# A hybrid encoder step in one core: transfers moved to GpSimd's queue, a third raw weight slot, and an input norm without GpSimd

## The chip, the cores and the metric

The kernel runs on one core of one Trainium2 chip. The core has a matrix engine (TensorE, "PE" in the profile, "PEld" its weight loads), VectorE (DVE), ScalarE (ACT), GpSimd (POOL) and SyncE (SP). Each of them takes its own instructions in order. Transfers between device memory and the core's on-chip memory are issued here from SP's and from POOL's instruction queues and run on 16 DMA engines. The metric is the device time of one execution in microseconds (us), as the median of several runs; lower is better.

## The reference

One layer of a streaming encoder, with the same weights for a prompt of 1024 frames and a sample of 32 frames. D is 1024, the MLP's hidden width 4096, the memory 256 tokens. Everything is float32.

```python
def trunk_layer(x, attn_core, conv_left, mem_k, mem_v, ...):
    h = rms_norm(x, g_mix)
    z = h @ w_in
    q, k, v, ch, cb, cc, ga, gb = jnp.split(z, SPLITS, axis=-1)
    a = attn_core(q, k, v) @ w_attn_out          # sliding window, sinks
    u = cc * ch
    ...                                          # conv: 3 taps over u
    bo = (cb * conv) @ w_conv_out
    x = x + (jax.nn.sigmoid(ga) * a + jax.nn.sigmoid(gb) * bo) @ w_mix_out
    hc = rms_norm(x, g_cross)
    cq = (hc @ w_cq).reshape(B, n, MEM_HEADS, MEM_HEAD_DIM)
    s = jnp.einsum('bqhd,bmhd->bhqm', cq, mem_k) * MEM_SCALE
    p = jax.nn.softmax(s, axis=-1)
    co = jnp.einsum('bhqm,bmhd->bqhd', p, mem_v).reshape(B, n, MEM_DIM)
    x = x + co @ w_co
    hm = rms_norm(x, g_mlp)
    x = x + jnp.square(jax.nn.relu(hm @ w_up)) @ w_down
    return x, k, v, up[:, -(CONV_WIDTH - 1):]
```

## The kernel before

The 1056 frames lie along the free axis in three chunks of 384, 384 and 288 (CH), the features along the partitions in eight tiles f of 128. Every float32 product is made of three matmuls: a weight is split into a high part `wh` (ACT, L119) and a low part `wl` (DVE, L120), activations into two such parts, and `gemm` (L175 to L177) sums high times high, high times low and low times high.

**Weights.** `fetch_w` (L135) loads the next weight in the program's list into one of two raw slots `wr` (SP, L137); `issue_w` (L141) splits it. For the weights in `kept`, the low part is also stored (`wl_d`, SP, L154) and loaded back (L148) for the next chunk.

**The start** is `norm_x`: x of the three chunks is loaded; `parts` makes X, the split of x times the norm's gain (`scaled_split`, ACT L255, DVE L256); `squares` sums the squares of the eight tiles in two halves, one on DVE (L313), one on POOL (L309 the squares of chunk 0, L313 the adds), and `column` merges them (L296). From the sums `chunk_col` makes the norm's factor per frame (L208 to L214), and `chunk_row` spreads it along the free axis (L222, L223, L225). K and V of a chunk are multiplied from X without the factor, then scaled (`v_scale`, L443, L412, L413). Then come Q of chunk 0 and the rest of attention. In the same time POOL starts the sums of w_down pieces (L739 load, L744 adds, L745 store), one after the other, up to 727 us.

**The trunk** (some 750 to 1080 us) goes chunk by chunk: `do_conv_out(c, f)` multiplies w_conv_out, loads the attention's part `m1` (SP) and adds it (L791); `do_mix(c, f)` loads x (L801, SP, into `ct`, a tag of six temporaries that many helpers share), multiplies w_mix and adds x (DVE, L805), makes the split of the sum (L255, L256) and its square (POOL L248, L252). The steps of cross-attention of the chunk before (scores, `turn`, `values` L916 to L931, `do_co` L943 to L947) and `normed_split` (L972, store L973) stand between the products of the next chunk.

**The MLP's up phase** (some 1080 to 1480 us). `up_part` multiplies one tile of w_up for one chunk, takes the positive part (DVE, L1000) and squares it (POOL, L1004). From 1220 us on `up_pair` makes a pair of tiles of chunks 0 and 1 by a Strassen-like scheme of fewer products: the sums of weights `s31` and `s24` are made on POOL (`pair_issue`, L1052 to L1055) and split (L119, L120); values are combined on POOL and DVE (L1111, L1136, L1145, L1154, L1162). Every value is put into the list `later`, and `flush` (L986) issues the stores on SP with the next product. In the down phase `pump` (L1206) and `refold` (L1217, L1221) load them again.

The order on each engine is made by a scheduler, which plays a timeline of the program and moves instructions within an engine; `pin` keeps some in the program's order, and within a `manual_schedule` block the order on the named engines is that of the code.

## Time and profile before

| | |
|---|---|
| runs | 1820.57, 1821.26, 1822.29 us (median 1821.26) |
| profiled execution | 1822.32 us |
| its span | 1820.5 us |
| TensorE busy | 1769.7 us (97%) |
| VectorE, ScalarE, GpSimd busy | 1110.2, 757.0, 531.4 us |
| mean granted TensorE clock | 0.99 |

The profile is of one execution; the span is from its first to its last recorded instruction. A row of a timeline has the start and the duration in us, the engine, the line, the operation and its tiles (out<-in), and in brackets the idle time before it with what ended it. A row of a group has the busy time and the mean in ns, then the idle time before the group. A row of waits has the total, the number and the longest, in us.

### The profile page before, as it was taken

How to read it: one execution, taken by the hardware profiler on the slowest of the kernel's cores; microseconds unless marked ns; L12 is line 12 of the kernel's file. 1: busy time of each engine (PE TensorE's matmuls, PEld its weight loads, DVE VectorE, ACT ScalarE, POOL GpSimd, SP SyncE). 2: the span in 40 equal slices, each digit the busy share in tenths (PEclk: the TensorE clock that was granted, in tenths of full speed). 3: DMA queues.
4: the chain of work that ended last, by engine and by line, in shares of the span. 5: the costliest groups of instructions: out<-in, count | busy, mean ns of one | idle time of the engine just before them, and what ended most of it. 6: DMA issues, size and time to landing. Idle time of an engine off the chain costs nothing. (4 is left out here: it accounts for less than half of the span.)

```text
span 1820.5 us, 29893 instructions
## 1 busy us (share of the span) xinstructions
PE 1769.7 (97%) x11172; PEld 1750.3 (96%) x11172; DVE 1110.2 (61%) x2083; ACT 757.0 (42%) x1486; POOL 531.4 (29%) x597
## 2 busy tenths in 40 slices
PE   7899999999999999999999989999999999999997
PEld 7899999999999999999999979999999999999997
DVE  7886766757665222425666768667566676436663
ACT  7553544535335210423465755632222343324453
POOL 4554310110113333002515142376544300100111
PEclk9999999999999999999999999999999999999999
DMA  6454411211126455516756657654334597446573
GB/s 224 161 175 150 149 56 53 80 56 63 61 93 199 148 174 183 163 55 210 242 197 214 225 191 251 241 189 140 133 125 138 160 295 223 156 128 205 193 241 105
DMA packets 166305, 293.35 MB, mean 161 GB/s; under 512 B 16624, under 2 KB 128016, under 8 KB 166032
## 3 DMA queue, kind: packets, MB, share of 16 engines
q1 hardware_dynamic: 156944, 257.88, 42.9%
q0 software_dynamic: 9216, 33.56, 5.2%
q8 instruction: 88, 1.44, 0.4%
q14 instruction: 57, 0.47, 0.1%
HBM read 217.89 MB, written 73.48 MB: 160 GB/s over the span
## 5 line engine op out<-in xcount | busy, mean ns | idle before, releaser
L175 PE MATMUL acc<-X,wh 128*128 128x384 f32 (+1 forms) x1200 | 392.1, 327 | 11.3 <-ACT wh L119 8.3
L176 PE MATMUL acc<-X,wh 128*128 128x384 f32 (+1 forms) x1200 | 389.0, 324 | 3.9 <-DVE X L256 3.9
L177 PE MATMUL acc<-X,wl 128*128 128x384 f32 (+1 forms) x1200 | 388.1, 323 | 0.4 <-DVE wl L120 0.4
L119 ACT CAST wh<-wr 128x1024 fp32r<-128x1024 f32 x208 | 218.2, 1049 | 361.1 <-PE acc L176 177.0
L120 DVE TENSOR_TENSOR wl<-wr,wh 128x1024 fp32r<-128x1024 f32 x208 | 274.3, 1319 | 99.8 <-ACT wh L119 98.7
L175 PEld LDWEIGHTS acc<-X,wh 128*128 128x128 f32 x1200 | 227.4, 189 | 12.0 <-ACT wh L119 8.3
L176 PEld LDWEIGHTS acc<-X,wh 128*128 128x128 f32 x1200 | 227.5, 190 | 4.9 <-DVE X L256 4.2
L177 PEld LDWEIGHTS acc<-X,wl 128*128 128x128 f32 x1200 | 227.2, 189 | 1.0 <-DVE wl L120 0.9
L175 PE MATMUL acc<-Y,wh 128*128 128x384 f32 (+1 forms) x624 | 202.4, 325 | 0.7 <-DVE ct L1000 0.4
L177 PE MATMUL acc<-Y,wl 128*128 128x384 f32 (+1 forms) x624 | 201.9, 324 | 0.0
L176 PE MATMUL acc<-Y,wh 128*128 128x384 f32 (+1 forms) x624 | 201.7, 323 | 0.0
L252 POOL TENSOR_TENSOR xacc<-xacc,ct 128x384 f32<-128x384 f32 (+1 forms) x62 | 76.5, 1237 | 319.3 <-ACT ct L250 314.2
L175 PEld LDWEIGHTS acc<-Y,wh 128*128 128x128 f32 x624 | 117.0, 188 | 1.4 <-DVE ct L1000 0.6
L176 PEld LDWEIGHTS acc<-Y,wh 128*128 128x128 f32 x624 | 117.1, 188 | 0.0
L177 PEld LDWEIGHTS acc<-Y,wl 128*128 128x128 f32 x624 | 117.1, 188 | 0.0
L1363 PE MATMUL acc<-Y,wh 128*128 128x384 f32 (+1 forms) x352 | 113.2, 322 | 1.3 <-DVE lt L1145 0.7
L1364 PE MATMUL acc<-Y,wh 128*128 128x384 f32 (+1 forms) x352 | 113.3, 322 | 0.6 <-DVE Y L120 0.6
L1365 PE MATMUL acc<-Y,wl 128*128 128x384 f32 (+1 forms) x352 | 113.0, 321 | 0.0
L119 ACT CAST PTh<-pt 128x512 fp32r<-128x512 f32 (+3 forms) x94 | 46.2, 516 | 124.5 <-PE pt L550 117.1
L120 DVE TENSOR_TENSOR Y<-ct,Y 128x384 fp32r<-128x384 f32 (+1 forms) x128 | 66.2, 549 | 42.3 <-ACT Y L119 42.1
L119 ACT CAST Y<-ct 128x384 fp32r<-128x384 f32 (+1 forms) x128 | 58.8, 486 | 59.0 <-DMA ct<-b_d 14.9
L1004 POOL TENSOR_TENSOR ct<-ct 128x288 f32<-128x288 f32 (+1 forms) x48 | 44.8, 934 | 120.3 <-DVE ct L1000 49.8
(309 smaller groups left out, 4192.5 us busy)
## 6 DMA issues: line engine op xcount, KB each, us to landing
wr<-in_w_in SPq DMA_DIRECT2D x50, 512.0 KB, 3.4
wr<-in_w_up SPq DMA_DIRECT2D x48, 512.0 KB, 3.9
wr<-in_w_down SPq DMA_DIRECT2D x32, 512.0 KB, 3.7
wr<-wsum_d SPq DMA_DIRECT2D x32, 512.0 KB, 3.5
wl<-wl_d SPq DMA_DIRECT2D x28, 512.0 KB, 4.8
wr<-in_w_conv_out SPq DMA_DIRECT2D x24, 512.0 KB, 4.2
wr<-in_w_mix SPq DMA_DIRECT2D x24, 512.0 KB, 4.2
ct<-b_d SPq DMA_DIRECT2D x48, 192.0 KB, 4.4
```

What stands on the lines that cost most here:

```text
L119: act.copy(hi, src)
L120: dve.tensor_sub(lo, src, hi.bitcast(F32))
L175: pe.matmul(out, wh[:, a], hi, start=(k == 0), stop=False)
L176: pe.matmul(out, wh[:, a], lo, start=False, stop=False)
L177: pe.matmul(out, wl[:, a], hi, start=False, stop=(k == len(acts) - 1))
L252: pool_e.tensor_tensor(acc, acc, sq, op=ALU.add)
L1004: pool_e.tensor_tensor(h, t, t, op=ALU.mult)
L1363: pe.matmul(a, wh[:, s], hi, start=(start and k == 0), stop=False, skip_group_check=True)
L1364: pe.matmul(a, wh[:, s], lo, start=False, stop=False, skip_group_check=True)
L1365: pe.matmul(a, wl[:, s], hi, start=False, stop=(stop and k == len(acts) - 1), skip_group_check=True)
```

## The change

Five things are changed. (a) Stores of the kept low parts go to POOL's queue. (b) The loads of m1 and x in the trunk go to POOL's queue, into four slots of their own (`ld`), and are asked for two products ahead (`add_next`). (c) Every third trunk weight goes into a third raw slot `wr3`. (d) At the start, all squares are on ACT (tag `sq`) and all adds on DVE (L307); ACT's and DVE's order for chunk 0 is written out, with the squares after the weights; splits of the later chunks are pinned; the scaling of a chunk's K and V comes after the next chunk's first V block, and that of the last chunk (`end`) after Q's first chunk. (e) Stores of `normed_split` and of `flush` go to POOL's queue. The numbers of lines in the changed kernel are up to 20 higher.

```diff
--- before.py
+++ after.py
@@ -129,10 +129,15 @@
             src = src[j]
         return src
 
-    fetched = []
+    fetched, trunk_raw, X = [], [0], {}
 
     def fetch_w():
-        raw = wp.tile([P, 1024], F32, tag="wr", bufs=2, name=nm("wr"))
+        name = worder[wpos[0] + len(fetched)][0]
+        trunk_raw[0] = trunk_raw[0] + 1 if name in ("w_conv_out", "w_mix", "w_cq", "w_co") else 0
+        if trunk_raw[0] % 3 == 1 and name in ("w_conv_out", "w_mix") and X:
+            raw = X["cr"].tile([P, 1024], F32, tag="wr3", name=nm("wr"))
+        else:
+            raw = wp.tile([P, 1024], F32, tag="wr", bufs=2, name=nm("wr"))
         src = weight(worder[wpos[0] + len(fetched)])
         sp.dma_start(raw.rearrange("p (i c) -> p i c", i=4) if len(src.shape) == 3 else raw, src)
         fetched.append(raw)
@@ -151,7 +156,7 @@
             split(hi, lo, raw)
             if key in kept:
                 kept[key] = dram.tile([P, 1024], F32, name=nm("wl_d"))
-                sp.dma_start(kept[key], lo.bitcast(F32))
+                pool_e.dma_start(kept[key], lo.bitcast(F32))
         ready.append((worder[wpos[0]], (hi, lo)))
         wpos[0] += 1
 
@@ -251,9 +256,9 @@
         if f:
             pool_e.tensor_tensor(acc, acc, sq, op=ALU.add)
 
-    def scaled_split(hi, lo, x, g):
-        act.mul(hi, x, col(g))
-        dve.scalar_tensor_tensor(lo, x, col(g), hi.bitcast(F32), op0=ALU.mult, op1=ALU.subtract)
+    def scaled_split(hi, lo, x, g, pinned=lambda x: x):
+        pinned(act.mul(hi, x, col(g)))
+        pinned(dve.scalar_tensor_tensor(lo, x, col(g), hi.bitcast(F32), op0=ALU.mult, op1=ALU.subtract))
 
 
     x_cm, xpool = opened("xpool", bufs=16)
@@ -264,6 +269,7 @@
         return st.tile([P, NF * 384], dt, tag="raw", bufs=3, name=nm("raw"))
 
     xg = [[None] * NF for _ in CH]
+    start_end = []
 
     def norm_x():
         pool_e.memset(ones, 1.0)
@@ -286,69 +292,72 @@
                     fetch_w()
                 raws.append(raw)
 
-        def parts(c, fs):
+        def parts(c, fs, pinned=lambda x: x):
             for f in fs:
                 xg[c][f] = (slot(xpool, f"X{c}", CH[c][1]), slot(xpool, f"X{c}", CH[c][1]))
-                scaled_split(*xg[c][f], raws[c][:, f], G_MIX + f)
-
-        def column(c):
-            a, b = accs[c]
-            dve.tensor_add(a, a, b)
-            accs[c] = [a]
-            chunk_col(c)
+                scaled_split(*xg[c][f], raws[c][:, f], G_MIX + f, pinned)
 
         def squares(c):
-
             n = CH[c][1]
-            sums = []
-            for e, h in ((dve, 0), (pool_e, 4)):
-                acc = st.tile([P, n], F32, tag=f"sum{h}", bufs=2 - h // 4, name=nm("sum"))
-                for f in range(h, h + 4):
-                    sq = acc if f == h else tmp(n)
-                    if c == 0 and h:
-                        pool_e.tensor_tensor(sq, raws[c][:, f], raws[c][:, f], op=ALU.mult)
-                    else:
-                        act.activation(sq, raws[c][:, f], AF.Square)
-                    if f > h:
-                        e.tensor_tensor(acc, acc, sq, op=ALU.add)
-                sums.append(acc)
-            accs[c] = sums
+            acc = st.tile([P, n], F32, tag="sum", bufs=2, name=nm("sum"))
+            for f in range(NF):
+                sq = st.tile([P, n], F32, tag="sq", bufs=2, name=nm("sq")) if f else acc
+                (pin if c and not f else lambda x: x)(act.activation(sq, raws[c][:, f], AF.Square))
+                if f:
+                    dve.tensor_add(acc, acc, sq)
+            accs[c] = [acc]
 
         with tc.manual_schedule(engines={mybir.EngineType.SP}):
             load_x()
-        parts(0, range(1))
-        issue_w()
-        parts(0, range(1, NF))
-        issue_w()
-        issue_w()
+        with tc.manual_schedule(engines={mybir.EngineType.Activation, mybir.EngineType.DVE}):
+            parts(0, range(2))
+            issue_w()
+            parts(0, range(2, NF))
+            issue_w()
+            issue_w()
+            squares(0)
         wk, wv = ready[0][1], (ready[1][1], ready[2][1])
         kt = at_tile([P, NT], F32, "kt")
         ktt[0] = kt
-        squares(0)
+        vs3 = {}
+
+        def scaled(c):
+
+            o, n = CH[c]
+            chunk_row(c)
+            k = kt[:, o : o + n]
+            pool_e.tensor_tensor(k, k, R[c], op=ALU.mult)
+            for j in range(3):
+                v_scale(vs3[c, j], c, j)
+
         for c, (o, n) in enumerate(CH):
             a = acc_tile([P, n])
             gemm(a, wk, xg[c])
-            k = kt[:, o : o + n]
-            act.copy(k, a)
-            v = [v_block(wv, c, j) for j in range(3)]
+            act.copy(kt[:, o : o + n], a)
             if c < 2:
-                parts(c + 1, range(NF))
-            column(c)
+                parts(c + 1, range(NF), pin)
+            vs3[c, 0] = v_block(wv, c, 0)
+            if c:
+                scaled(c - 1)
+            chunk_col(c)
+            vs3[c, 1] = v_block(wv, c, 1)
+            vs3[c, 2] = v_block(wv, c, 2)
             if c < 2:
                 squares(c + 1)
-            chunk_row(c)
-            pool_e.tensor_tensor(k, k, R[c], op=ALU.mult)
-            for j in range(3):
-                v_scale(v[j], c, j)
             if c == 1:
                 mem_load_x()
-        sp.dma_start(io["o_k"][0], kt[:, 896:])
-        v = tmp(256)
-        sp.dma_start(v, io["cache_v"])
-        vtile(v)
         for key in start_keys:
             next_w(key)
-        dve.tensor_scalar_mul(nsink, prm[:, SINK0 : SINK0 + 20], -1.0)
+
+        def end():
+            scaled(2)
+            sp.dma_start(io["o_k"][0], kt[:, 896:])
+            v = tmp(256)
+            sp.dma_start(v, io["cache_v"])
+            vtile(v)
+            dve.tensor_scalar_mul(nsink, prm[:, SINK0 : SINK0 + 20], -1.0)
+
+        start_end.append((0, end))
 
     mrc = st.tile([P, 2], F32, name="mrc")
     mr = st.tile([P, 256], F32, name="mr")
@@ -640,7 +649,7 @@
     start_keys = [("w_in", 8), ("w_v", 0), ("w_v", 1)]
     worder.extend(start_keys)
     item(norm_x)
-    item(do_Q(0, 0), qt(0, 0))
+    item(do_Q(0, 0, start_end), qt(0, 0))
     item(mem_keys(0), ("w_ckv_k", 0))
     item(mem_keys(1), ("w_ckv_k", 1))
     item(mem_values, ("w_ckv_v", 0), ("w_ckv_v", 1))
@@ -766,6 +775,7 @@
 
     mpool = ctx.enter_context(tc.tile_pool(name="mpool", bufs=16, reuse_waits="tile"))
     cr_cm, cr = opened("cross", bufs=1, reuse_waits="tile")
+    X["cr"] = cr
     mg = [[None] * NF for _ in CH]
     x1 = [[None] * NF for _ in CH]
     xc = [[None] * NF for _ in CH]
@@ -779,11 +789,22 @@
         scaled_split(hi, lo, x, g)
         return hi, lo
 
+
+    adds = [(src, c, f) for c in range(3) for src in ("m1", "x") for f in range(NF)]
+    added = []
+
+    def add_next():
+        while adds and len(added) < 3:
+            src, c, f = adds.pop(0)
+            t = cr.tile([P, 384], F32, tag="ld", bufs=4, name=nm("ld"))[:, : CH[c][1]]
+            pool_e.dma_start(t, (m1_d[c] if src == "m1" else io[f"x{c}"])[:, f])
+            added.append(t)
+        return added.pop(0)
+
     def do_conv_out(c, f):
         def fn(w):
             n = CH[c][1]
-            t1 = tmp(n)
-            sp.dma_start(t1, m1_d[c][:, f])
+            t1 = add_next()
             a = acc_tile([P, n])
             gemm(a, w, bcp[c])
             t = tmp(n)
@@ -797,8 +818,7 @@
     def do_mix(c, f):
         def fn(w):
             n = CH[c][1]
-            xt = tmp(n)
-            sp.dma_start(xt, io[f"x{c}"][:, f])
+            xt = add_next()
             a = acc_tile([P, n])
             gemm(a, w, mg[c])
             x = gate_slot(c, f)
@@ -970,7 +990,7 @@
     def normed_split(c, f):
         t = tmp(CH[c][1])
         pin(dve.scalar_tensor_tensor(t, x1[c][f], col(G_MLP + f), R[c], op0=ALU.mult, op1=ALU.mult))
-        sp.dma_start(xn_d[c][:, f], t)
+        pool_e.dma_start(xn_d[c][:, f], t)
         hi, lo = xm[c][f] = (yslot(c), yslot(c))
         act.copy(hi, t)
         pin(dve.tensor_sub(lo, t, hi.bitcast(F32)))
@@ -983,7 +1003,7 @@
 
     def flush():
         for args in later:
-            sp.dma_start(*args)
+            pool_e.dma_start(*args)
         later.clear()
 
     def hidden(c, j, h):
```

What stands on VectorE at the start before, from the second split of x on (X are the splits, wl the weights' low parts, sum the sums of squares):

```order
L256 SCALAR_TENSOR_TENSOR X_12_154<-raw_122,prm,X_11_153 128x384
L120 TENSOR_TENSOR wl_150<-wr_125,wh_149 128x1024
L256 SCALAR_TENSOR_TENSOR X_14_158<-raw_122,prm,X_13_157 128x384
L313 TENSOR_TENSOR sum_190<-sum_190,ct_195 128x384
L256 SCALAR_TENSOR_TENSOR X_16_162<-raw_122,prm,X_15_161 128x384
L313 TENSOR_TENSOR sum_190<-sum_190,ct_198 128x384
L256 SCALAR_TENSOR_TENSOR X_18_166<-raw_122,prm,X_17_165 128x384
L256 SCALAR_TENSOR_TENSOR X_20_170<-raw_122,prm,X_19_169 128x384
L256 SCALAR_TENSOR_TENSOR X_22_174<-raw_122,prm,X_21_173 128x384
L120 TENSOR_TENSOR wl_182<-wr_130,wh_181 128x1024
L256 SCALAR_TENSOR_TENSOR X_24_178<-raw_122,prm,X_23_177 128x384
L120 TENSOR_TENSOR wl_186<-wr_132,wh_185 128x1024
```

And with the change, from the second split on:

```order
L261 SCALAR_TENSOR_TENSOR X_10_152<-raw_122,prm,X_9_151 128x384
L120 TENSOR_TENSOR wl_156<-wr_125,wh_155 128x1024
L261 SCALAR_TENSOR_TENSOR X_14_160<-raw_122,prm,X_13_159 128x384
L261 SCALAR_TENSOR_TENSOR X_16_164<-raw_122,prm,X_15_163 128x384
L261 SCALAR_TENSOR_TENSOR X_18_168<-raw_122,prm,X_17_167 128x384
L261 SCALAR_TENSOR_TENSOR X_20_172<-raw_122,prm,X_19_171 128x384
L261 SCALAR_TENSOR_TENSOR X_22_176<-raw_122,prm,X_21_175 128x384
L261 SCALAR_TENSOR_TENSOR X_24_180<-raw_122,prm,X_23_179 128x384
L120 TENSOR_TENSOR wl_184<-wr_130,wh_183 128x1024
L120 TENSOR_TENSOR wl_188<-wr_132,wh_187 128x1024
L307 TENSOR_TENSOR sum_191<-sum_191,sq_193 128x384
L307 TENSOR_TENSOR sum_191<-sum_191,sq_196 128x384
```

The adds between the splits are gone from there; all of the chunk's follow its third weight.

GpSimd in the last stretch of single up products, up to the end of the second pair's sums of weights (L1054 before, L1074 now; s are the sums, ct the squared values, M and Y operands of the pairs). Before:

```order
L1111 TENSOR_TENSOR xacc_8850<-xacc_8850 128x384
L1052 TENSOR_TENSOR s_2508_13546<-wr_2476_13306 128x512
L1055 TENSOR_TENSOR s_2508_13546<-wr_13305,wr_2476_13306 128x512
L1004 TENSOR_TENSOR ct_13483<-ct_13481 128x288
L1053 TENSOR_TENSOR s_2509_13547<-wr_13305,s_2508_13546 128x512
L1004 TENSOR_TENSOR ct_13543<-ct_13541 128x288
L1054 TENSOR_TENSOR s_2509_13547<-wr_13305,s_2509_13547 128x512
```

And now:

```order
L1072 TENSOR_TENSOR s_2508_13549<-wr_2476_13309 128x512
L1075 TENSOR_TENSOR s_2508_13549<-wr_13308,wr_2476_13309 128x512
L1024 TENSOR_TENSOR ct_13486<-ct_13484 128x288
L1006 DMA hid_d<-ct_13452 128x288
L1053 TENSOR_TENSOR Y_2460_13229<-lt_13207,Y_2459_13228 128x384
L1006 DMA b_d<-xacc_8853 128x384
L1024 TENSOR_TENSOR ct_13546<-ct_13544 128x288
L1073 TENSOR_TENSOR s_2509_13550<-wr_13308,s_2508_13549 128x512
L1131 TENSOR_TENSOR xacc_8853<-xacc_8853 128x384
L1006 DMA hid_d<-ct_13486 128x288
L1006 DMA hid_d<-ct_13546 128x288
L1074 TENSOR_TENSOR s_2509_13550<-wr_13308,s_2509_13550 128x512
```

Four stores, of squared values and of a pair's value, stand between these operations; further up, from the squared value `ct_13010` on, eight more stand among its like.

The loads of x for the last tiles of chunk 2 in the trunk. SyncE before (wr are raw weights, wl the kept low parts, xn_d the stores of `normed_split`):

```order
L973 DMA xn_d_86<-ct_11300 128x384
L137 DMA wr_11588<-in_w_co 128x1024
L801 DMA ct_11409<-in_x 128x288
L137 DMA wr_11636<-in_w_mix 128x1024
L973 DMA xn_d_86<-ct_11396 128x384
L148 DMA wl_11591<-wl_d_10450 128x1024
L137 DMA wr_11678<-in_w_up 128x1024
L801 DMA ct_11484<-in_x 128x288
L973 DMA xn_d_86<-ct_11445 128x384
L801 DMA ct_11545<-in_x 128x288
L973 DMA xn_d_86<-ct_11520 128x384
```

And GpSimd with the change (L800 is `add_next`, L253 and L257 are the squares and their adds, L993 the stores of `normed_split`):

```order
L800 DMA ld_11367<-in_x 128x288
L800 DMA ld_11416<-in_x 128x288
L253 TENSOR_TENSOR ct_11304<-Ga_1982_11298 128x288
L257 TENSOR_TENSOR xacc_8853<-xacc_8853,ct_11304 128x288
L993 DMA xn_d_86<-ct_11258 128x384
L253 TENSOR_TENSOR ct_11400<-Ga_2008_11394 128x288
L800 DMA ld_11491<-in_x 128x288
L257 TENSOR_TENSOR xacc_8853<-xacc_8853,ct_11400 128x288
L993 DMA xn_d_86<-ct_11307 128x384
L253 TENSOR_TENSOR ct_11449<-Gb_2020_11443 128x288
L800 DMA ld_11552<-in_x 128x288
L993 DMA xn_d_86<-ct_11403 128x384
```

The last load stands behind the square of `Gb_2020`; three more products of w_mix are added to x before the one that it serves.

## The prediction

> **What bounds the kernel now.** I read the page's busy shares first, then TensorE's waits in four stretches, then what the other engines do there.
>
> ```profile
> span 1820.5 us, 29893 instructions
> PE 1769.7 (97%) x11172; PEld 1750.3 (96%) x11172; DVE 1110.2 (61%) x2083; ACT 757.0 (42%) x1486; POOL 531.4 (29%) x597
> ```
>
> TensorE (PE) is the bound: 97% busy, 50.8 us of idle in the whole span. The change takes no matmul away that matters, so it can gain only what lies in that idle time and in stretches at a lower clock. The busy times of each engine in the stretches that matter, with the granted clock as the third number from the end:
>
> ```profile
> core 0: us, PE busy (x) PEld busy (x) DVE busy (x) ACT busy (x) POOL busy (x), PEclk, DMA share, GB/s
> 0.00:8.30 8.30, 0.03 (x1) 0.03 (x1) 1.88 (x5) 6.14 (x10) 2.65 (x10) 1.00 0.80 287
> 8.30:31.10 22.80, 18.45 (x102) 17.51 (x103) 19.93 (x22) 13.09 (x27) 10.71 (x12) 0.85 0.86 318
> sum 62.60, PE 45.72 PEld 44.31 DVE 49.74 ACT 44.53 POOL 33.22; mean PE 11.43 PEld 11.08 DVE 12.44 ACT 11.13 POOL 8.31
> 1000.00:1040.00 40.00, 40.00 (x295) 39.93 (x294) 29.04 (x59) 27.07 (x58) 5.79 (x6) 1.00 0.67 227
> 1040.00:1080.00 40.00, 32.24 (x184) 28.78 (x183) 29.48 (x47) 21.93 (x39) 21.61 (x20) 0.91 0.60 197
> 1200.00:1240.00 40.00, 37.50 (x225) 36.95 (x224) 26.74 (x32) 12.42 (x19) 28.37 (x24) 0.96 0.34 106
> 1240.00:1280.00 40.00, 40.00 (x250) 40.00 (x249) 26.25 (x34) 10.19 (x12) 23.97 (x19) 1.00 0.46 157
> ```
>
> Two stretches carry most of what can be gained: the start (to 62.6 us PE is idle for 62.6 - 45.7 = 16.9 us) and the end of the trunk, 1040 to 1080 (7.8 us idle, and 0.09 x 40 = 3.6 us lost to the clock). Just before it, from 1000 to 1040, PE is full: nothing saved there shows.
>
> **The start.** PE's longest wait after its first, and what stands on VectorE (DVE) and GpSimd (POOL) then:
>
> ```profile
> 17.28 0.69 PE L176 MATMUL acc<-X,wh 128*128 128x384 f32 x1 [3.93 <-DVE X L256]
> 12.11 4.58 DVE L313 TENSOR_TENSOR sum<-sum,ct 128x384 f32<-128x384 f32 x1
> 16.62 1.67 DVE L256 SCALAR_TENSOR_TENSOR X<-raw,prm,X 128x384 fp32r<-128x384 f32 x3
> 12.94 2.38 POOL L309 TENSOR_TENSOR ct<-raw 128x384 f32<-128x384 f32 x3
> L313 DVE TENSOR_TENSOR sum<-sum,ct x6: 548/558/4583, 5.1 to 33.5; 128x384 f32<-128x384 f32 x6
> ```
>
> One add of the square sums took 4.58 us where its median is 0.56, from 12.11 to 16.6, beside POOL's squares (the row shown runs from 12.9 to 15.3); three splits of x queued behind it and PE with them. The change takes POOL out, and puts all adds of chunk 0 behind its splits and its three weights. So the wait of 3.93 goes, and up to 0.15 x 22.8 = 3.4 us of half clock with it: chunk 0's K and V end 3.9 to 7.3 us earlier.
>
> Given back: DVE gets 21 adds in place of 9 and 3 merges, 9 more at 0.56 us = 5.0 us, and ScalarE (ACT) 4 squares. DVE is busy 49.7 of the first 62.6 us. It loses 4.58 - 0.56 = 4.0 and gains 5.0, so 50.7 us; before its first weight (8.3 us) it did only 1.88 us, so 6.4 us of its idle cannot be used. Were it solid from there, the first product of Q could come at 50.7 + 6.4 = 57.1 instead of 62.6: 5.5 us sooner. Chunk 2's splits also stand behind memory splits on ACT now, so I don't take the whole of it: **-5 us** (0 to -7.3).
>
> **Residual loads two products ahead.** The loads of x for the last mix products, and who waits:
>
> ```profile
> 1059.91 0.46 DVE L805 TENSOR_TENSOR Gb<-acc,ct 128x288 f32<-128x288 f32 x1 [1.70 <-DMA ct<-in_x]
> 1070.10 0.46 DVE L805 TENSOR_TENSOR Gb<-acc,ct 128x288 f32<-128x288 f32 x1 [2.98 <-DMA ct<-in_x]
> DVE Gb L805 <- DMA ct<-in_x: 4.7, 2, 3.0
> DVE Ga L805 <- DMA ct<-in_x: 1.7, 1, 1.7
> PE acc L943 <- DVE Gb L805: 2.4, 3, 1.5
> PE o L916 <- DVE tO L919: 1.7, 1, 1.7
> SPq L973 <- DVE ct L972: 12.4, 5, 4.6
> L801 SPq DMA_DIRECT2D ct<-in_x x24: 368/424/2072, 860.4 to 1072.8; - x24
> DMA to landing us min/median/max: 3.3/4.9/6.5
> wr<-in_w_mix SPq DMA_DIRECT2D x2, 512.0 KB, 4.7
> ```
>
> From 1040 to 1075 DVE stands 4.7 + 1.7 = 6.4 us still for x, which SyncE (SP) issued late, behind stores (L973) that wait for DVE themselves, and which takes 4.9 us to land. PE's waits in that stretch end with DVE products for the most part. Asked for two products earlier, x is there. DVE then runs up to 6.4 us ahead of where it was; not each of these reaches PE (DVE is busy only 29.5 of 40), but less idle also keeps the clock up. Bounds: nothing, if another DVE operation is late next, and 7.8 + 3.6 = 11.4 us. I take **-6**, near DVE's own 6.4. The m1 loads of the trunk's products and chunks 0 and 1 gain nothing: PE is full at 1000 to 1040. The kept weight stores and the third raw slot are there too: 0, covered by that full PE; without the cover the most would be one weight landing, 4.7 us, once or twice.
>
> What POOL takes over there: an issue on POOL costs as the w_down sums show:
>
> ```profile
> L745 POOL DMA_DIRECT2D wsum_d<-xacc x16: 576/590/608, 11.5 to 219.8; - x16
> 219.75 0.58 POOL L745 DMA_DIRECT2D wsum_d<-xacc  x1 [0.41 <-POOL xacc L744]
> wsum_d<-xacc POOLq DMA_DIRECT2D x16, 512.0 KB, 3.1
> ```
>
> So 0.59 us of POOL per transfer, and 0.41 more where it follows its own operand's operation; a store lands after 3.1 us. In 1040 to 1080 POOL is busy 21.6 of 40 and gets some 10 such: 5.9 us, room enough.
>
> The SBUF page of the Trainium skill ("SBUF — State Buffer", Who interferes with whom) speaks against such a move: a transfer issued from GpSimd can be kept waiting while VectorE holds the shared port pair, and it should go to SyncE's queue. The 16 issues above span 576 to 608 ns with DVE at work around them, so these rows don't show it. [...]
>
> **Stores of the MLP, into POOL's order.** Between 1182 and 1224 the pair sums for the Strassen products run on POOL, with this end:
>
> ```profile
> 1219.64 0.66 POOL L1004 TENSOR_TENSOR ct<-ct 128x288 f32<-128x288 f32 x1
> 1222.13 1.26 POOL L1054 TENSOR_TENSOR s<-wr,s 128x512 f32<-128x512 f32 x1
> 1223.42 1.04 ACT L119 CAST wh<-s 128x1024 fp32r<-128x1024 f32 x1 [4.47 <-POOL s L1054]
> 1224.52 0.58 PE L1070 MATMUL acc<-hx,wh 128*128 128x384 f32 x1 [1.91 <-ACT wh L119]
> L1004 POOL TENSOR_TENSOR ct<-ct 128x288 f32<-128x288 f32 x11 | 10.8, 985 | 9.3 <-issue 7.5 <-DVE ct L1000 1.8
> L1026 POOL TENSOR_TENSOR lt<-lt,lt 128x384 f32<-128x384 f32 x4 | 4.3, 1079 | 2.9 <-DVE lt L1025 1.6 <-DMA lt<-xn_d 1.3
> ```
>
> PE waits 1.91 us for a sum that POOL finishes at 1223.4, and POOL is nearly solid from 1182 on (between its operations some 4.7 us: 1.8 for DVE after the first, 2.9 before L1026). The change puts 12 stores ahead of that same sum: 12 x 0.59 = 7.1 us. If all the 4.7 us of gaps take some, 2.4 us remain; if none, 7.1. PE is late by as much. I take **+4** (0 to +7.1; zero if stores fall only where POOL waited). The half clock that follows such a wait (0.04 x 40 = 1.6 us) is paid already.
>
> In the steady pairs, 1240 to 1440, where PE is full in the window shown, one of the pair sums, and the end of the sums of one pair:
>
> ```profile
> L1053 POOL TENSOR_TENSOR s<-wr,s 128x512 f32<-128x512 f32 x9 | 17.8, 1979 | 0.0
> 1301.79 1.05 ACT L119 CAST wh<-s 128x1024 fp32r<-128x1024 f32 x1 [1.57 <-PE pa L176]
> 1297.24 0.83 POOL L1111 TENSOR_TENSOR xacc<-xacc 128x384 f32<-128x384 f32 x1
> L986 SPq DMA_DIRECT2D n_d<-lt x36: 319/319/408, 1239.4 to 1470.6; - x36
> DMA to landing us min/median/max: 1.7/2.5/6.6
> ```
>
> Nine sums in 200 us, a tenth begun, make a pair of some 21 us. POOL is busy 24.0 of 40 there, 12.6 a pair; nine stores a pair add 9 x 0.59 = 5.3, and with 0.41 at each 9.0. That makes 18 to 21.6 of 21: full or nearly. The last sum (done at 1297.2, where L1111 starts) is cast at 1301.8, when PE frees the slot: 4.5 us of slack, against 3 or 4 stores of delay (2.4 to 4 us) in the chain of sums. Hidden: **0**, but only just (at the upper end 0.6 x 9 = 5 us). The end of the up phase (1440 to 1480, where values are read back) could shift by 3 us either way with loads that no longer queue behind stores, and a store that lands 3.1 us after its issue where SP's stores of L986 took 2.5: 0.
>
> **Sum.** -5 - 6 + 4 = -7 on a span of 1820.5, so 1813.5, and 1.8 around it (1822.3 profiled): 1815.3. The profiled run lies 1.1 above the median of 1821.26, so **1814.3 us**.
>
> **The rivals.** One row that the third of them needs:
>
> ```profile
> L120 DVE TENSOR_TENSOR wl<-wr,wh 128x1024 fp32r<-128x1024 f32 x208 | 274.3, 1319 | 99.8 <-ACT wh L119 98.7
> ```
>
> (1) *POOL becomes the pace of the MLP's up phase* (slower). For it: 18 to 21.6 of 21 us by the sum above, in order, and stores that wait for DVE hold the sums behind them. Against: PE-paced slack of 4.5 us. It decides as soon as a pair needs over 21 us of POOL: at 0.41 more per issue (1.41 us each, 12.6 + 9 x 1.41 = 25.3) it would lose 4.3 us for each of 9 pairs, 39 us: 1853. Just past the point (22 a pair) it is 9 us, and with the sum at 1224 at its upper price (+3), 1814 + 12 = 1826.
> (2) *The gains are hidden anyway.* At the start, chunk 2's splits behind the memory splits and a DVE that is nearly solid let Q start only 1 to 2 us sooner; at 1060 the next DVE product (L919, 1.7 us of PE's waits) is late in place of x, and leaves 2. Then -2 - 2 + 4 = 0: 1821.
> (3) *POOL's issues wait out DVE's operations.* Nine stores a pair, each later by one DVE weight split (1.32 us), give 12.6 + 9 x 1.91 = 29.8 of 21 us: 8.8 x 9 = 79 us, 1893. [...]
> (4) *The stores cost nothing* (they fall where POOL waits for DVE), and the clock stays up: -7 - 8 = -15, 1806.
>
> **Chances.** Forecast 0.50, (1) 0.19, (2) 0.16, (3) 0.04, (4) 0.11. A measurement here tells 0.2% (3.6 us) from no change. Faster (below 1817.6): the forecast but for its upper tail, (4) and a little of (2): 0.60. Same: most of (2) and that tail: 0.16. Slower: (1), (3) and the rest of (2): 0.24. The range takes in (4) below and the near side of (1) above: 1804 to 1828; the forecast's own is 1808 to 1820.
>
> **What would show it.** Start right: no wait over 2 us between 9 and 30 us, Q's first matmul at 56 to 59. Loads right: no DVE wait for in_x after 1040, and PE busy at least 36 of the 40 us that were 1040 to 1080. Stores right: a PE wait of 4 to 8 us for ACT's cast of s near the old 1224, none in the steady pairs. Wrong, if PE waits for ACT casts of s in each pair (rival 1), or if POOL's issues last over 1 us (rival 3), or if the first product of Q still waits past 60 us (rival 2).

## The result, and the profile after

| | before | changed |
|---|---|---|
| median of four runs each, same chip | 1821.33 us (1820.57 to 1822.29) | 1837.08 us (1835.56 to 1838.62) |
| span of the profiled execution | 1820.5 us | 1833.9 us |
| mean granted clock | 0.99 | 0.99 |

The ratio is 1.0086, with a 95% interval of 1.0069 to 1.0104: the change makes the kernel slower by 15.7 us. The first page lines of the changed kernel:

```profile
span 1833.9 us, 29866 instructions
PE 1773.4 (97%) x11172; PEld 1752.6 (96%) x11172; DVE 1137.4 (62%) x2092; ACT 758.7 (41%) x1490; POOL 623.3 (34%) x794
```

PE's idle time went from 50.8 to 60.5 us. Both kernels run 11172 matmuls, in the same order but for some stretches (20 to 75 us and 1225 to 1348 above all), so the n-th matmul of one can be set against the n-th of the other. The start of each such pair, changed less before, gives a balance by stage (stages in the time of before; inside such a stretch it is rough):

| stage | forecast | measured | a part alone |
|---|---|---|---|
| start to 110 | -5 | +1.8 (-6.3 at 31, -2.3 at 82) | d: +2.8 |
| 797 to 830, last gates, first w_conv_out | 0 | +4.1 | c: +4.1 |
| 840 to 985 | 0 | +1.6 | a: +1.9 |
| 1026 to 1097, residual loads | -6 | -1.8 | b: -2.2, -2.8 |
| 1097 to 1131, scores of the last chunk | 0 | +2.4 | not isolated |
| 1163 to 1244, MLP stores | +4 | +2.0 (+4.9 at 1208) | e: +3.3 |
| 1244 to 1440, steady pairs | 0 | +0.9 | e: +0.9 |
| 1440 to 1500, end of the up phase | 0 | +2.4 | c +3, d +3, e +4 |
| sum | -7 | +13.4 | |

A profile is of one execution. How far two of them lie apart is seen in those kernels below that leave a stage as it was in before. They differ from before's profile by -1.1 to +2.2 us at the start (the first matmul itself comes at 8.1 to 10.6 us), by -0.2 to +0.9 at 840 to 985, by -1.8 to +0.2 at 1026 to 1097, by -0.1 to +0.6 at 1097 to 1131, by -2.0 to +1.5 at 1163 to 1244 and by -1.4 to +5.5 at 1440 to 1500, and by nothing at 797 to 830 and 1244 to 1440. So the start's +1.8 says only that the forecast gain is not there, the loads' -1.8 and the last stage's +2.4 are not clear of this spread, and the +4.1, the +2.4 at the scores and the +0.9 are.

The busy times by stretch answer to those of the prediction:

```profile
8.30:31.10 22.80, 22.20 (x148) 21.69 (x149) 18.62 (x32) 17.76 (x37) 6.75 (x8) 1.00 0.86 321
31.10:62.60 31.50, 24.59 (x167) 24.18 (x167) 25.84 (x46) 23.96 (x63) 18.61 (x24) 0.84 0.23 84
1040.00:1080.00 40.00, 33.89 (x204) 31.26 (x203) 32.94 (x53) 24.00 (x45) 24.23 (x27) 0.87 0.55 183
1240.00:1280.00 40.00, 39.60 (x245) 38.95 (x244) 31.95 (x32) 10.50 (x12) 35.03 (x38) 1.00 0.45 150
```

In the first stretch PE does 148 matmuls at full clock where it did 102 at 0.85: the stall of 3.93 us is gone. The next stretch, at a clock of 0.84, gives all of it back. Between 82 and 93 us another 4.0 are lost: PE waits 1.10, 1.22 and 0.92 us for the memory's norm, where before has the last of these waits and one of 0.18, and its clock is 0.84 there in place of 1.00. Over the first 110 us the mean clock is 0.94 in both kernels: the half clock that the first stretch saved comes back behind later waits. From 1240 POOL is busy 35.0 of 40 (24.0 before), and PE still 39.6: rival 1 did not come.

PE's longest waits in the changed kernel, as rows of its timeline (line numbers of the changed kernel; L190 is the product of V, L336 the copy of K, L452 and L1006 the scaling of V and `flush`, L229 the memory's norm row, L963 `do_co`, L900 the scores, L1020 the positive part of an up product, L1090 a product of the pairs, L1384 the down phase):

```profile
40.02 0.58 PE L190 MATMUL acc<-wh,X 128*128 128x256 f32 x1 [5.17 <-ACT kt L336]
56.69 0.39 PE L190 MATMUL acc<-wh,X 128*128 128x256 f32 x1 [1.74 <-ACT kt L336]
84.60 0.39 PE L229 MATMUL pr<-ct,ones_r 128*128 128x256 f32 x1 [1.10 <-ACT ct L227]
828.89 0.44 PE L180 MATMUL acc<-Y,wh 128*128 128x384 f32 x1 [1.96 <-ACT wh L119]
1061.69 0.69 PE L963 MATMUL acc<-Y,wh 128*128 128x384 f32 x1 [1.65 <-DVE Gb L825]
1125.71 0.39 PE L900 MATMUL sc<-mkh,Y 128*128 128x256 f32 x1 [1.66 <-ACT mkh L119]
1192.10 0.40 PE L180 MATMUL acc<-Y,wh 128*128 128x288 f32 x1 [2.43 <-DVE ct L1020]
1208.77 0.66 PE L1090 MATMUL acc<-Y,wh 128*128 128x384 f32 x1 [3.41 <-DVE ct L1020]
1486.86 0.40 PE L1384 MATMUL acc<-H,wh 128*128 128x288 f32 x1 [3.32 <-DVE H L120]
```

**At 40 us** PE waits for ScalarE's copy of K of chunk 1. Five of ScalarE's rows, the last of them that copy:

```profile
32.13 0.53 ACT L305 ACTIVATE sq<-raw 128x384 f32<-128x384 f32 x1 [1.57 <-DVE sum L307]
33.22 1.31 ACT L452 ACTIVATE ct<-ct,rc 128x256 f32<-128x256 f32 x3 [0.56 <-DVE rc L219]
34.44 2.08 ACT L260 ACTIVATE raw<-raw,prm 128x256 fp32r<-128x256 f32 x5
37.45 0.90 ACT L260 ACTIVATE raw<-raw,prm 128x256 fp32r<-128x256 f32 x2
39.50 0.46 ACT L336 COPY kt<-acc 128x384 f32<-128x384 f32 x1
```

A square waits for VectorE to free its slot, then come chunk 0's scaling and eight splits of the memory, which nobody needs yet. PE had been idle since 34.9; K's copy starts at 39.5, and V's next product has no accumulator until then.

**At 829 us** SyncE shows why a third slot made weights later:

```profile
782.97 41.12 SPq L142 DMA_DIRECT2D wr<-in_w_conv_out  x3
SPq L142 <- PE acc L182: 28.8, 1, 28.8
```

Three loads stand as one row of 41 us. The second line, of SyncE's waits from 780 to 830, tells why: one of them waits 28.8 us for a matmul, until 823.7, when the gates' last matmul of 384 frames ends, and what is behind it in SP's order is held too. Before, the same loads wait only for a raw slot to be split (the first two stand in a row that begins at 792.7):

```profile
SPq L137 <- DVE wl L120: 33.4, 3, 11.1
```

**At 1125 us** PE waits for the memory's keys (`mkr`, two loads of 64 KB). Their issue and the time to their landing, before and changed:

```profile
1113.25 1.16 SPq L816 DMA_DIRECT2D mkr<-in_cmem_k  x2
DMA to landing us min/median/max: 3.1/3.2/3.3
```

```profile
1118.18 2.25 SPq L836 DMA_DIRECT2D mkr<-in_cmem_k  x2
DMA to landing us min/median/max: 5.9/6.1/6.2
```

They are issued 4.9 us later, but PE is 6.2 us later by then, so the issue is not what is late: they take 6.1 us to land in place of 3.2. In the changed kernel a w_up weight, a kept low part and four other stores are issued, on two queues, within 4.5 us around them, and the DMA engines are busy for 0.97 of 1118.2 to 1125.2; before, for 0.81 of 1113.3 to 1117.0. That this crowd makes the landing long is a reading, not shown.

### The profile page after: what moved, and what is told of

Its sections match the earlier page's. It is cut to its first block, busy times and chain, and to the rows that moved or that the text cites. A ratio compares the mean times of both kernels' runs of the same rounds, so it can differ in the third digit from the quotient of the medians.

```text
span 1833.9 us, 29866 instructions
## 1 busy us (share of the span) xinstructions
PE 1773.4 (97%) x11172; PEld 1752.6 (96%) x11172; DVE 1137.4 (62%) x2092; ACT 758.7 (41%) x1490; POOL 623.3 (34%) x794
## 4 chain that ended last, share of the span: by engine, by line
PE 80%; DMA 7%; DVE 6%; issue 3%; ACT 2%; POOL 1%; SPq 0%; DVEq 0%; POOLq 0%; ACTq 0%
PE acc L180 15%; PE acc L182 15%; PE acc L181 15%; PE acc L1384 5%; PE acc L1385 5%; PE acc L1383 5%; PE acc L1092 3%; PE acc L1090 3%; PE acc L1091 3%; PE pt L559 1%; DVE wl L120 1%; DMA ct<-b_d 1%; PE pa L181 1%; PE pa L182 1%; PE pa L180 1%
## 5 line engine op out<-in xcount | busy, mean ns | idle before, releaser
L120 DVE TENSOR_TENSOR wl<-wr,wh 128x1024 fp32r<-128x1024 f32 x208 | 283.2, 1363 | 111.2 <-ACT wh L119 108.3
L257 POOL TENSOR_TENSOR xacc<-xacc,ct 128x384 f32<-128x384 f32 (+1 forms) x62 | 72.3, 1167 | 319.4 <-ACT ct L255 317.9
L1384 PE MATMUL acc<-Y,wh 128*128 128x384 f32 (+1 forms) x352 | 113.9, 323 | 0.9 <-DVE Y L120 0.9
L753 POOL TENSOR_TENSOR ws<-ws 128x256 f32<-128x256 f32 x64 | 56.1, 876 | 60.6 <-DMA ws<-in_w_down 56.8
```

Of the source, the lines that this page charges most:

```text
L120: dve.tensor_sub(lo, src, hi.bitcast(F32))
L257: pool_e.tensor_tensor(acc, acc, sq, op=ALU.add)
L753: pool_e.tensor_tensor(t[:, to], t[:, x], t[:, y], op=ALU.add)
L1384: pe.matmul(a, wh[:, s], lo, start=False, stop=False, skip_group_check=True)
```

## The experiments

Each kernel is timed against before on the same chip. Before's medians were 1821.05 (e1 to e4), 1820.63 (e5 to e8), 1821.98 (e9 to e12), 1820.96 (e13 to e16) and 1824.31 (e17, e18). The ratio is an estimate of its own and need not be the quotient of the two medians. Line numbers in the rows are those of each run's own kernel. The profiled execution is one of the runs and can lie far from the median: e12's is the fastest of 11 (1820.85), e15's the second slowest of 6 (1833.45).

| run | what | median us | ratio, 95% interval |
|---|---|---|---|
| e1 | c alone | 1827.56 | 1.0040, 1.0028 to 1.0052 |
| e2 | d alone | 1827.01 | 1.0037, 1.0025 to 1.0049 |
| e3 | e alone | 1828.68 | 1.0045, 1.0029 to 1.0060 |
| e4, e16 | b alone, twice | 1819.92, 1818.14 | 0.9995, 0.9986 to 1.0004; 0.9983, 0.9975 to 0.9992 |
| e13 | a alone | 1823.98 | 1.0022, 1.0010 to 1.0034 |
| e5 | c, another third weight | 1823.16 | 1.0007, 0.9996 to 1.0018 |
| e6 | d, memory splits pinned | 1827.17 | 1.0040, 1.0025 to 1.0055 |
| e7 | d, `end` not put off | 1826.20 | 1.0022, 1.0010 to 1.0034 |
| e8, e15 | `flush` alone, twice | 1828.52, 1827.85 | 1.0052, 1.0038 to 1.0066; 1.0044, 1.0029 to 1.0058 |
| e9 | `flush`, from the first pair on | 1825.06 | 1.0014, 1.0002 to 1.0025 |
| e10 | d, memory's load and splits later | 1826.47 | 1.0027, 1.0015 to 1.0040 |
| e11 | all, slot as in e5 | 1832.96 | 1.0061, 1.0040 to 1.0082 |
| e12 | b, c as in e5, d as in e10 | 1826.94 | 1.0030, 1.0017 to 1.0042 |
| e14 | before again | 1821.62 | 1.0004, 0.9996 to 1.0013 |
| e17 | before, banks shifted | 1825.94 | 1.0011, 1.0002 to 1.0020 |
| e18 | e8, banks shifted | 1831.49 | 1.0044, 1.0030 to 1.0057 |

### Each part alone

e1 is before with the third slot only, e2 with the start only, e3 with both kinds of stores on POOL (`normed_split` and `flush`), e4 with the loads only, e13 with the stores of kept low parts only; their diffs are the hunks of the change.

> The kernel before with the third raw slot alone (part c). Theory of places: the slot lies in a pool whose memory the gates' x operands used, so the first w_conv_out weight can be loaded only after the last gate matmul; PE waits some 2 us for ScalarE's cast near 826 us, and half clock follows: +4.1 us, 1825.4. Rival (all of the loss is the stores in GpSimd's order): within 1 us of before.

> The kernel before with the new start alone (part d). Theory of places: 6.4 us ahead by 33 us, all lost by 110 us, because ScalarE's copy of K of chunk 1 stands behind the memory splits and chunk 0's V scaling: +1.8 us, 1823.1. Rival (stores are all of it): the start gains as predicted, -5 us, 1816.

> The kernel before with the stores of normed_split and flush on GpSimd's queue alone (part e). Theory of places: +2 us between 1160 and 1240, +2 in the pairs, +2.4 at the end of the up phase: +4 to +7, about 1827. Rival (stores are all of it): +14 us or more, 1835.

> The kernel before with the loads of m1 and x on GpSimd's queue, two products ahead, alone (part b). Theory of places: VectorE no longer waits for x at 1040 to 1075, -2 to -4 us, 1818. Rival (stores are all of it): the full -6 us of the prediction, 1815.

> Part (a) alone: the stores of the kept low parts on GpSimd's queue, all else as before. Theory (the nine stores' place is a detail): 1820 to 1823, the same as before; a wait of at most 1 us for a wl read back near 900, as the changed kernel had at 902.62 (0.84), since a 512 KB store lands after 5.2 us there in place of 3.0. Rival (any edit to the program moves the scheduler's order and costs some us at the end of the up phase): +3 to +6 between 1450 and 1490 though no code there is changed, 1824 to 1827. The sum over parts (+6.5, +6.0, +7.6, -1.1 for c, d, e, b against +15.7 for all) leaves about -3 for (a) if parts add up.

Only (b) does not lose. The ratios add up to more than the whole (0.22 + 0.40 + 0.37 + 0.45, less 0.11 for b, is 1.33%, against 0.86%): e1, e2 and e3 each count a loss of 3 to 4 us at the end of the up phase, which the whole change has once.

e1 has the changed kernel's wait of 1.96 at 827.79 and its +4.1. e2 is 5.3 us ahead at 28 us and has lost it all by 60: waits for K's copy of 4.69 and 2.60, then three of about 1 us near 86; +2.8 at 108. In e3 the weights' sum at 1224 is not late. PE loses earlier, at 1182.82 (2.52) and 1200.02 (2.41), both behind VectorE; of its +5.8 there, 2.5 come back at 1224, since the sum is done by then. VectorE (L1031 makes M) and POOL of e3 near 1196, and the same M of before in the last row:

```profile
1195.37 4.13 DVE L1031 TENSOR_TENSOR M<-lt,M 128x384 fp32r<-128x384 f32 x1
...
1195.60 1.30 POOL L1053 TENSOR_TENSOR s<-wr,s 128x512 f32<-128x512 f32 x1
1196.84 1.02 POOL L1033 TENSOR_TENSOR M<-lt,M 128x384 fp32r<-128x384 f32 x1
1197.81 1.27 POOL L1055 TENSOR_TENSOR s<-wr,wr 128x512 f32<-128x512 f32 x1
```

```profile
1193.98 1.37 DVE L1031 TENSOR_TENSOR M<-lt,M 128x384 fp32r<-128x384 f32 x1
```

One VectorE operation takes 4.13 us, and ends at 1199.5, 0.4 us after a solid run of three POOL operations (1195.6 to 1199.1); the next value that PE waits for is queued behind it. The changed kernel has the same at 1204.15, 4.10 us.

e4 has no DVE wait for x left (6.4 us before). What ends PE's waits from 1040 to 1085 there:

```profile
PE acc L952 <- DVE Gb L814: 2.0, 2, 1.6
PE acc L953 <- DVE Y L940: 1.5, 1, 1.5
```

The sum with x (L814) now waits for its own product, not for x, and behind it come the splits of Y. PE does 34.3 of 40 us (32.2 before), at a clock of 0.87 in place of 0.91 (the clock itself varies: e14, before again, has 0.87 there, and e16, this kernel again, 0.91). The stage is 2.2 us shorter than in before's profile, 2.8 in e16; kernels that leave these loads alone are up to 1.8 shorter too, so the gain is nearer to 1 or 2 us.

e13 loses 1.9 us from 840 to 985, up to 0.9 of which unchanged kernels lose too: near 982 SyncE brings x later, and PE waits 1.39 us for its sum.

```profile
982.68 0.56 DVE L805 TENSOR_TENSOR Gb<-acc,ct 128x384 f32<-128x384 f32 x1 [6.43 <-DMA ct<-in_x]
```

Before, VectorE waited 5.14 us for that x and PE waited 0.29 there, for another product. The stores of low parts landed after a median of 3.0 us from SyncE's queue, and of 5.2 from GpSimd's in the changed kernel. That x is late because the read of a low part, one place ahead on SP, waits for a store that lands 2 us later is a reading, not shown.

### The third slot

```diff
-        if trunk_raw[0] % 3 == 1 and ...
+        if trunk_raw[0] % 3 == 0 and ...
```

> The kernel before with the third raw slot, but taken by every third trunk weight from the third on, so the first two w_conv_out weights use the old slots. If the loss near 826 us is the slot's memory (still read by the gates' last matmul when the first weight should be loaded), the 4.1 us there vanish: 1823.5, some 3 us of it at the end of the up phase. If a third slot itself costs (its loads collide with others), it stays near 1827.6.

> The changed kernel with the third slot taken from the third trunk weight on. If the parts add up, PE's wait near 826 us goes and with it 4 us: 1833 (2 to 6 us under the change). If the wait only moves to the late loads of m1 or to the next weight: 1836 to 1838.

e5 moves the third slot's first use from the first w_conv_out to the third. The wait at 827 and the loss vanish (1.0007), also in the whole change: e11's median is 4.1 us below the change's (the two intervals overlap, but its profile loses 0.0 at 797 to 830), and PE has no such wait near 829. Its gain elsewhere is nil. With the 28.8 us that the load waits for a matmul, this shows the slot's loss: its memory is not free until the gates' matmuls are through, and SP holds everything behind it.

### The start

```diff
 e6
-                act.copy(kt[:, o : o + n], a)
+                pin(act.copy(kt[:, o : o + n], a))
-            scaled_split(*mact[f], mx[:, f], G_MEM + f)
+            scaled_split(*mact[f], mx[:, f], G_MEM + f, pin)
 e7
-        start_end.append((0, end))
+        end()
...
-    item(do_Q(0, 0, start_end), qt(0, 0))
+    item(do_Q(0, 0), qt(0, 0))
 e10: as e6, and
-            if c == 1:
-                mem_load_x()
...
+        mem_load_x()
         for key in start_keys:
```

> The new start alone, with the memory splits pinned behind the splits of chunk 2 and the copy of K pinned. If ScalarE's order makes PE wait at 34 to 44 us, the wait of some 5 us for the copy of K shrinks by the eight memory splits, some 3.5 us, and the time from 1827.0 to 1823.5. If chunk 2 is bound by its own splits on VectorE, the gain is lost by 60 us and the time stays at 1826 to 1827.

> The new start alone, with the scaling of the last chunk's K and V done before Q again instead of inside it. If its deferral makes the waits at 83 to 88 us (3.2 us for the identity times the norm's factor), they vanish: 1827.0 to about 1823.5. If the same work only stands elsewhere in the queue, PE waits for it before Q and the time stays at 1827.

> The new start alone, with the memory's load and splits issued behind chunk 2 and pinned there, and the copies of K pinned. If ScalarE's order is what gives the start's gain back, the waits for the copies of K (5 us at 35 and 2.7 at 55) shrink to 1.5 us together and PE is 2 to 4 us ahead of before at 108 us: 1817 to 1819, or 5 us more where the end of the up phase comes out in its slower form. If VectorE bounds the start, as the forecast's own sum of 57 us says, Q comes no sooner and the time is 1821 or more.

In e6 the first wait for K's copy falls from 4.69 to 1.51, as expected of ScalarE's order. But the memory splits are now ahead of chunk 2's copy, and PE waits there; at 108 e6 is +0.4 where e2 was +2.8:

```profile
38.49 0.39 PE L185 MATMUL acc<-wh,X 128*128 128x256 f32 x1 [1.51 <-ACT kt L331]
53.55 0.61 PE L176 MATMUL acc<-X,wh 128*128 128x288 f32 x1 [1.86 <-DVE X L256]
58.00 0.58 PE L185 MATMUL acc<-wh,X 128*128 128x256 f32 x1 [2.75 <-ACT kt L331]
```

e10 keeps the memory out of the way until chunk 2 is through: 1.35 and 1.42 us remain of the waits for K, Q's first product comes at 56.0 us (62.6 before), and then the products behind are late. The first of these waits ends with the scaling of Q (L464), which frees an accumulator; on VectorE it stands behind the eight splits of the memory and three values. The second is for the memory's norm:

```profile
65.73 5.15 DVE L256 SCALAR_TENSOR_TENSOR raw<-raw,prm,raw 128x256 fp32r<-128x256 f32 x8
74.08 0.55 PE L175 MATMUL acc<-raw,wh 128*128 128x256 f32 x1 [5.32 <-DVE ct L464]
87.42 0.58 PE L224 MATMUL pr<-ct,ones_r 128*128 128x256 f32 x1 [2.66 <-ACT ct L222]
```

It is +4.6 at 93 (2.2 of it was there at the first matmul, which starts anywhere from 8.1 to 10.6 us in these runs). e7 is 2.8 to 3.9 us ahead from 65 to 82 and loses it to the memory's norm at 84.34 (2.26): +2.0 at 108. In all of them ScalarE is busy for 59.7 to 60.4 of the first 90 us (58.2 before), VectorE for 64.0 to 66.2 (69.3 before). As these rows read, nearly the same work has to be done before 90 us, and each order moves the wait to the next product that needs some of it; a better order was not ruled out. No version here kept chunk 0's gain.

### The stores

```diff
 e8: flush alone on POOL
 e9:
-            sp.dma_start(*args)
+            (pool_e if pairs else sp).dma_start(*args)
...
     def up_start():
+        flush()
+        pairs.append(1)
```

> The kernel before with only the stores of flush on GpSimd's queue (those of normed_split stay on SyncE's). If GpSimd's order and its hold on VectorE in 1180 to 1240 are the loss, nearly all of it stays: 1827 to 1829. If the stores of normed_split, which wait in GpSimd's queue for VectorE, are the loss: back to 1822.

> The kernel before with the stores of flush on GpSimd's queue only from the first pair on; the single up products store on SyncE as before. Theory of places: the 6 us lost at 1180 to 1210 go, the steady pairs cost under 1 us, and what is left is the end of the up phase: 1821 to 1826. Rival (GpSimd's time in the steady pairs is the pace, the first rival of the prediction): 5 us or more between 1240 and 1440, 1827 or more.

e8 (1.0052) has all of e3's loss (1.0045), so it is `flush`, not the stores of `normed_split`. Its wait at 1182.91 (3.12, for DVE ct L1000) goes back to the norm's row R, and ScalarE of e8 shows why that is late:

```profile
1173.11 1.05 ACT L149 CAST wh<-wr 128x1024 fp32r<-128x1024 f32 x1 [2.91 <-PE acc L176]
...
1175.47 0.20 ACT L209 ACTIVATE st_s<-st_v 128x3 f32<-128x3 f32 x1
...
1180.83 1.04 ACT L149 CAST wh<-wr 128x1024 fp32r<-128x1024 f32 x1 [2.21 <-DMA wr<-in_w_up]
1181.89 0.40 ACT L235 COPY R<-pr 128x288 f32<-128x288 f32 x1
```

And in before:

```profile
1174.03 0.20 ACT L209 ACTIVATE st_s<-st_v 128x3 f32<-128x3 f32 x1 [0.29 <-DVE st_v L208]
1174.98 1.05 ACT L149 CAST wh<-wr 128x1024 fp32r<-128x1024 f32 x1 [0.74 <-PE acc L176]
```

In e8 two casts of weights stand ahead, one of the norm's root, one of the copy of R, each waiting for something else; in before the root began at 1174.03, with the cast behind it. The scheduler moved them, though the edit names neither.

e9 leaves `flush` on SP until the pairs begin: the loss at 1180 to 1210 goes, and from 1240 to 1440 the change against before is 0.0 us with nine stores a pair on POOL. The pairs hide them.

### The end of the up phase

From 1440 to 1500 e3, e6 and e8 lost 2.8 to 5.5 us, e6 with no code changed near there. In these three PE's wait is the same to the hundredth; here the row of e3:

```profile
1470.09 0.66 PE L1363 MATMUL acc<-Y,wh 128*128 128x384 f32 x1 [6.08 <-DVE lt L1159]
```

```diff
 e14, e15, e16 (before, e8 and e4 with):
-        after("W3")
         h21 = lt()
         dve.tensor_sub(h21, B, s1)
+        after("W3")
```

> Before with one edit at the end of a pair: the difference h21 (B - s1, which reads the last product out of its accumulator) is written ahead of the step W3 in place of behind it. Theory (the waits at 1452 and 1461 are for the accumulator that h21 or h12 holds, behind splits on VectorE): before's own waits there, 3.35 and 0.74, become shorter or stay; 1818 to 1822. Rival (the order shifts elsewhere, as with any edit): a change of +-3 at places with no connection, 1818 to 1826.

> Stores of flush on GpSimd (as in e8, 1828.5) and h21 written ahead of W3. Theory (the 6.08 us wait at 1461 in three variants is the last down accumulator's slot, freed only by the last h21, which stands behind three or four splits of M on VectorE): the wait of 6.08 goes or falls below 3, and the time is 3 to 5 us under e8: 1823.5 to 1825.5; what is left over before (about +4) is the loss at 1180 to 1210. Rival (6.08 is set by the stores on GpSimd's queue, as by s or hidden values that are late): it stays at 5 to 6 and the time is within 1 us of e8.

> Part (b) alone, as in e4 (1819.9, ratio 0.9995), with h21 written ahead of W3. Theory: e4's -2.3 at 1040 to 1080 is kept and its +1.9 at the end of the up phase goes: 1817 to 1819, faster than before by 0.1 to 0.2%. Rival (that +1.9 has nothing to do with h21): 1819.5 to 1821.

This edit changed nothing: in the built programs every engine's order is that of before, e8 and e4. The three runs are repeats: e14 tells how far two profiles of one program lie apart (up to 1.7 us, at 1208 to 1240; e4 and e16, one program too, lie 2.4 apart at 1440 to 1500), e15 has the 6.08 again, and e16 makes (b) faster by 0.17%, on the same program that gave 0.05% in e4.

In the built programs the first accumulator of the down phase lies in bank 0 of PSUM, the accumulators' memory, each time. In before, C of the last pair held that bank; in e3, e6 and e8, B did, and B is read by h21 (L1159), behind splits on VectorE. e17 and e18 move the down phase's accumulators by two banks and no instruction:

```diff
         n_acc = 6
+        ps.tile([P, 384], F32, tag="pt", bufs=2, name=nm("pt"))
```

> Before with the accumulators of the down phase moved by two banks of PSUM (a tile that nothing uses stands ahead of them in their pool), every instruction in the same place in its engine's order. In the built program the first down accumulator then lies in bank 2, which the last pair's B held, in place of bank 0, which C held. Theory (whose bank it gets decides the wait at 1461): it must wait for h21 = B - s1, which VectorE makes at 1467.5 behind five splits of M, in place of h12 at 1462.2: the wait of 0.74 becomes about 6.1, PE is 5 us later from there, and the time is 1824 to 1826. Rival (the bank doesn't matter, the wait is for VectorE's order): 0.74 stays, 1820 to 1822.

> e8 (stores of flush on GpSimd, 1828.5) with the same shift by two banks and no instruction moved. There B lies in bank 0 and C in bank 2, so that the shift gives the first down accumulator C's bank. Theory: the wait of 6.08 becomes 0.3 to 1.5 (h12 at 1461.5), and the time is 4 to 5 us under e8: 1823 to 1825; what is left is the loss at 1180 to 1210. Rival (stores on GpSimd's queue make it): 6.08 stays, 1828.

The same matmul in before, e17 and e18:

```profile
1462.86 0.41 PE L1363 MATMUL acc<-Y,wh 128*128 128x384 f32 x1 [0.74 <-DVE lt L1145]
```

```profile
1468.97 0.66 PE L1364 MATMUL acc<-Y,wh 128*128 128x384 f32 x1 [6.08 <-DVE lt L1159]
```

```profile
1466.80 0.42 PE L1364 MATMUL acc<-Y,wh 128*128 128x384 f32 x1 [0.74 <-DVE lt L1145]
...
1482.23 0.40 PE L1365 MATMUL acc<-H,wh 128*128 128x288 f32 x1 [1.94 <-DVE H L120]
```

The bank alone puts the 6.08 into before and takes it out of e8, as the theory had it. The time follows little. e17 loses 4.2 us in this stage of its profile, but 1.6 us in the medians; that its 1825.94 lies in the expected range owes much to a before that is 3 us slower on this chip (1824.31), where no profile of it was taken. e18 keeps a loss of 4.9 us in the stage, and its ratio is no better than that of e15: the wait is gone, and three for H, the values read back, stand in its place (1.94, 1.01 and 1.05). The changed kernel has that form too (3.32, 0.84 and 1.02 at 1486 to 1490), and e10 (1.19, 1.21 and 0.70), whose stores are on SP. In e18 ScalarE waits 5.21 us for such a value, until 1483.7:

```profile
1483.70 0.43 ACT L119 CAST H<-ct 128x288 fp32r<-128x288 f32 x1 [5.21 <-DMA ct<-hid_d]
```

So two things can end this stage, the bank and the values read back, and mending the one left the other. e1 and e2 lose 3.2 and 3.4 us here with the wait of 0.74: they have two waits for H (1.52 and 0.90; 1.01 and 0.90) where before has one of 1.01, and a mean clock from 1440 to 1500 of 0.94 and 0.91 where before has 0.97. Why H is later there stays open.

### All that could be mended

> The start of the run before, the loads of m1 and x on GpSimd's queue and the third slot from the third weight on; all stores on SyncE. The sum of the places: -2 to -4 at the start, -2 at 1040 to 1080, 0 for the slot: 1815 to 1817, below both kernels, if the end of the up phase keeps the form that it has before; 1820 to 1822 if it does not.

e12 is b, the late slot and e10's start, with all stores on SP. Its profile is 1.5 us ahead after the trunk, but that execution is its fastest; by its runs it is slower than before (1.0030). PE waits 3.45 at 69.84 and 2.60 at 84.40 at its start, as in e10. The best kernel of the study is (b) alone, 0.05% and 0.17% faster in two measurements, of which only the second is clear of the noise.

## Why the prediction was wrong

It said 1814.3 us, faster; it was 1837.1. By its terms, on the span: -7 forecast, +13.4 measured, 20.4 apart. The bound was read rightly (PE stays 97% busy), and so were the waits that the change removes; what failed is what came in their place.

**The start, -5: +1.8.** Its first half held: no wait over 2 us from 9 to 30, and chunk 0's products 6.3 us sooner (3.9 to 7.3 were given). The step that failed is "VectorE solid from 8.3 us, the first product of Q at 57.1": it counted VectorE's busy time and took order on ScalarE for a remark ("chunk 2's splits also stand behind memory splits"). The same in-order queue holds K's copy, and two waits of 5.17 and 1.74 follow: Q's first product came at 61.0, 1.5 us sooner than before, as rival 2 had it. In e10, with that order mended, it comes at 56.0, so the sum for VectorE was within reach. But the term took Q for the end of the start. The memory's splits and norm have to be through before 90 us, and no term held them: 4.0 us go there in the changed kernel, and e10 goes from 6.8 us ahead at 65 to 4.6 behind at 93.

**The loads, -6: -1.8** (e4: -2.2, and part of either is before's own profile). The mechanism held, with no wait for x left. The term was mis-sized, in the way rival 2 put it: another VectorE or ScalarE product is late next. PE was busy 33.9 of 40, not 36, and the idle taken from VectorE did not keep the clock: 0.87, against 0.91 before and 0.87 when before was run again.

**The third slot, 0: +4.1.** "Covered by that full PE" looked at where the slot helps, not at which memory it lies in. It is the largest single loss, and the wait of 28.8 us with e5 and e11 show its cause.

**Kept stores, 0: +1.6** over the stage, and 1.9 in e13, of which up to 0.9 is the spread of profiles; e11, with the same stores on POOL, has +0.3. The bound named was one landing of 4.7 us, once or twice. By e13's runs (1.0022) the value taken, nothing, was too low, but where it is lost in the whole change is not shown.

**The MLP stores, +4: +2.0** (e3: +3.3). The sign held, and the size came near by luck, since the mechanism was another: not the weights' sum at 1224 but two waits before it, from casts that the scheduler put ahead of the norm, and from a VectorE operation held beside POOL. This loss and that at the scores don't add: e11 loses 4.7 at the scores and gains 1.3 behind them, and from 1097 to 1244 together every kernel with all of `flush` on POOL loses 2.9 to 4.4. Pairs 0: +0.9, and 0.0 in e9: hidden, and rival 1 with them. POOL's load was forecast well (18 to 21.6 of 21 us a pair; 35.0 of 40 are 18.4), and PE does not wait for it. Rival 3 fell too: no run shows an issue that waits out a VectorE operation. The loads of x on POOL in the changed kernel, with the shortest, median and longest issue in ns:

```profile
L800 POOL DMA_DIRECT2D ld<-in_x x24: 536/566/596, 858.2 to 1053.3; - x24
```

The port rule of the Trainium skill's SBUF page ("SBUF — State Buffer", Who interferes with whom), by which a transfer issued from GpSimd can wait while VectorE holds the shared port pair in a two-port mode, shows nowhere in these rows, and by the same section `tensor_tensor`, the form of the weight split by which rival 3 was priced, has no such mode. That the two engines hold each other in computing does show, in the 4.13 us above.

**What no term held:** the scores at 1097 to 1131 (+2.4), where the memory's keys landed 6.1 us after their issue in place of 3.2, a loss that needs the parts together (e3 and e4 have 0.1 and -0.1 there, e13 0.9, e11 4.7); and the end of the up phase (+2.4 in the whole, up to 5.5 in parts), which was set at 0 within 3 either way.

## What to carry to other kernels

An operation moved from one in-order queue to another changes what stands behind what on both: read the built order for what is now ahead of the next needed value (here K's copy behind splits that nobody needed yet), and for each queue name the first instruction that will wait. A load can be issued in time and still land late, so compare the time to landing as well. An added prefetch slot is only early if its memory is free early; otherwise it holds the queue for all that follows. Where a scheduler and a pool choose order and banks, count a few us for stages that no edit touches, and read a part's worth stage by stage, since the same loss can show in every variant and not add up.
